# Storing one row of the first tile ahead, through Pool's queue, in a softmax bound by DMA

## The chip, the cores and the metric

One core of a Trainium2 chip. The names are the profile's: DVE is the vector engine, ACT the scalar engine, Pool (POOL) GpSimd and SP the sync engine; SBUF is the memory on the chip, HBM the memory that holds input and output. A transfer is cut into pieces, each one packet record of the trace, which 16 DMA engines move. The metric is device microseconds of one execution, as the median of several; runs of this kernel agree within about 0.3%.

## The reference

```python
x = np.random.randn(32, 512, 1024).astype(np.float32)      # temperature = 0.5
scaled = x / temperature
shifted = scaled - np.max(scaled, axis=-1, keepdims=True)
exp_x = np.exp(shifted)
return exp_x / np.sum(exp_x, axis=-1, keepdims=True)
```

67.1 MB are read and 67.1 MB written, so 134.2 MB must pass the DMA engines, however the arithmetic is done.

## The kernel before

The 16384 rows are cut into 16 tiles of 1024 rows, eight on each of 128 partitions. The eight rows of a partition lie together in HBM and in SBUF, so a whole tile moves in pieces of 32 KiB, and one row of every partition (128 x 4 KiB, 0.52 MB) in pieces of 4 KiB. There are six buffers. SP issues the loads, ACT the stores; a load into a used buffer waits for the store out of it. A tile is computed in "groups" of rows: the first two and last two tiles in two groups of four, the others in one of eight.

```python
def load():
    i = len(tiles)
    if i < len(PASSES):
        xt = data.tile([P, ROWS, d], f32, name="xt")     # data: 6 buffers
        nc.sync.dma_start(out=xt, in_=dram(xf, i))
        tiles.append(xt)

# maximum(g):     DVE reduces the rows of group g to their maxima (L68)
# exponential(g): ACT, row by row, exp and its sum (L77)
# divide(g):      DVE, reciprocal of the sums, then row by row (L95) or whole (L92)

def store(g):
    i, a, k = groups[g]
    if a + k == ROWS:                                    # the tile's last group
        nc.scalar.dma_start(out=dram(of, i), in_=tiles[i])
        load()

for _ in range(BUFS):
    load()
for g in range(len(groups) + 1):
    # ... cut: the last two tiles divide and store ahead of the next maximum
    maximum(g); exponential(g)
    divide(g - 1); store(g - 1)
```

## Time and profile before

| What | Value | Where it is from |
|---|---|---|
| time | 317.11 us, 317.06 to 317.88 in 3 runs; 317.26 us in 6 | the runs |
| DMA queues' busy share | 49.8% loads + 49.2% stores | the page, DMA queues |
| steady DMA rate | 432 to 433 GB/s | busy time by stretches, 60 to 280 us |
| one piece of 32 KiB on one of 16 engines | 1.213 us, 256 on each: 310.5 us | packet records of the trace |
| fullest compute engine | DVE, 79% | the page, busy time |

Read it from the DMA row. A kernel whose transfers run at one rate from the first to the last microsecond has a time of "bytes over rate, plus two ends", and what an engine does beside them matters only where it leaves the transfers without work.

Two sums from the records of data packets: **Slow packets** is the time that pieces took beyond their usual duration (1.213 us for 32 KiB, 1.062 for 28, 0.611 for 16, 0.159 for 4), summed and divided by 16 engines. **Idle** is the time between the first and the last data packet less the time of these packets over 16. In the kernel before they are 2.08 and 0.45 us: 310.53 + 2.08 + 0.45 = 313.06 us, from 1.73 to 314.79.

### The profile page before, as it was taken

Reading aid. Unit: us, or ns where it says so; the run is one execution under the profiler, and the core shown is the slowest. Engines: PE = TensorE matmul, PEld = TensorE weight load, DVE = VectorE, ACT = ScalarE, POOL = GpSimd, SP = SyncE. Lnnn points to the kernel's source line nnn. Section 1 sums busy time; section 2 is a strip of 40 time slices with the busy share of each in tenths; the row PEclk is TensorE's granted clock in tenths of the full one; section 3 lists DMA queues with packets and bytes.
Section 4 is the critical chain, followed back from the end, with each engine's and each line's share of the span. In section 5 each row is a group of like instructions: output and inputs, shape, how many; then the busy total and the mean of one; then the engine's idle time right before and its main releaser. Section 6 shows DMA issues by size and latency. Waiting matters only on the chain. (4 is left out here: it accounts for less than half of the span.)

```text
span 316.0 us, 530 instructions
## 1 busy us (share of the span) xinstructions
DVE 251.0 (79%) x146; ACT 148.1 (47%) x257; POOL 0.2 (0%) x4
## 2 busy tenths in 40 slices
DVE  0399999999689794997939979299793999979710
ACT  0176637680907428083380924708247091564700
POOL 0000000000000000000000000000000000000000
DMA  8999999999999999999999999999999999999996
GB/s 328 415 448 423 377 456 407 460 403 456 408 452 415 452 402 444 419 452 411 452 415 452 427 436 432 431 436 427 436 427 448 415 448 419 448 415 456 407 456 282
DMA packets 4611, 134.24 MB, mean 425 GB/s; under 512 B 512, under 2 KB 512, under 8 KB 512
## 3 DMA queue, kind: packets, MB, share of 16 engines
q1 hardware_dynamic: 2304, 67.11, 49.8%
q10 hardware_dynamic: 2304, 67.11, 49.2%
q14 instruction: 3, 0.02, 0.0%
HBM read 67.11 MB, written 67.11 MB: 425 GB/s over the span
## 5 line engine op out<-in xcount | busy, mean ns | idle before, releaser
L77 ACT ACTIVATE xt<-xt,bias 128x1024 f32<-128x1024 f32 x128 | 145.1, 1135 | 136.7 <-DVE bias L71 127.2
L68 DVE TENSOR_REDUCE top<-xt 128x8 f32<-128x8192 f32 (+1 forms) x20 | 139.5, 6976 | 44.6 <-DMA xt<-in_x_dram 44.6
L95 DVE TENSOR_SCALAR xt<-xt,recip 128x1024 f32<-128x1024 f32 x80 | 54.3, 749 | 0.5
L92 DVE TENSOR_TENSOR xt<-xt,recip 128x8192 f32<-128x8192 f32 x6 | 52.2, 8692 | 0.2
L77 ACT ACTIVATION_READ_ACCUMULATOR xt<-xt,bias 128x1 f32 x128 | 23.8, 186 | 0.0
L77 ACT ACT_TABLE_LOAD x1 | 1.3, 1283 | 13.3 <-DMA xt<-in_x_dram 13.3
L89 DVE RECIPROCAL recip<-sums 128x8 f32<-128x8 f32 (+1 forms) x20 | 3.7, 187 | 4.1 <-ACT xt L77 4.1
L71 DVE TENSOR_SCALAR bias<-top 128x8 f32<-128x8 f32 (+1 forms) x20 | 3.4, 170 | 0.7
L138 POOL MEMSET const-bfloat16-1.0<- 128x1 bf16 x1 | 0.1, 101 | 0.0
L138 POOL MEMSET const-uint8-127<- 128x1 uint8 x1 | 0.1, 101 | 0.0
L138 POOL MEMSET const-float32-0.0<- 128x1 f32 x1 | 0.1, 98 | 0.2 <-issue 0.2
L138 POOL MEMSET const-float32-1.0<- 128x1 f32 x1 | 0.1, 98 | 0.0
## 6 DMA issues: line engine op xcount, KB each, us to landing
xt<-in_x_dram SPq DMA_DIRECT2D x16, 4096.0 KB, 49.7
out_dram<-xt ACTq DMA_DIRECT2D x16, 4096.0 KB, 29.5
```

Source lines behind the costliest of these rows:

```text
L68: nc.vector.tensor_reduce(out=top, in_=tiles[i][:, a : a + k, :], axis=mybir.AxisListType.X, op=extreme)
L71: nc.vector.tensor_scalar_mul(bias, in0=top, scalar1=-scale)
L77: nc.scalar.activation(tiles[i][:, a + b, :], tiles[i][:, a + b, :], mybir.ActivationFunctionType.Exp, bias=bias[:, b : b + 1], scale=scal ...
L89: nc.vector.reciprocal(recip, sums)
L92: nc.vector.tensor_mul(xt, xt, recip.unsqueeze(2).to_broadcast([P, k, d]))
L95: nc.vector.tensor_scalar_mul(tiles[i][:, a + b, :], in0=tiles[i][:, a + b, :], scalar1=recip[:, b : b + 1])
L138: nc = _bacc.Bacc("TRN2", target_bir_lowering=False, num_devices=1)
```

## The change

The intent: until 33 us only loads run, and the first group of the first tile is finished at 25 us. The first row of each partition, 0.52 MB, is stored then, through a third queue, so that writing begins sooner. ACT stores the other seven rows where it stored all eight.

```diff
     def store(g):
         i, a, k = groups[g]
-        if a + k == ROWS:
-            nc.scalar.dma_start(out=dram(of, i), in_=tiles[i])
+        if g == 0:
+            nc.gpsimd.dma_start(out=dram(of, i)[:, :1, :], in_=tiles[i][:, :1, :])
+        elif a + k == ROWS:
+            a = 1 if i == 0 else 0
+            nc.scalar.dma_start(out=dram(of, i)[:, a:, :], in_=tiles[i][:, a:, :])
             load()
```

## The prediction

> **What bounds the kernel now.** I read the head of the page first: which engine is full?
>
> ```profile
> DVE 251.0 (79%) x146; ACT 148.1 (47%) x257; POOL 0.2 (0%) x4
> DMA  8999999999999999999999999999999999999996
> GB/s 328 415 448 423 377 456 407 460 403 456 408 452 415 452 402 444 419 452 411 452 415 452 427 436 432 431 436 427 436 427 448 415 448 419 448 415 456 407 456 282
> q1 hardware_dynamic: 2304, 67.11, 49.8%
> q10 hardware_dynamic: 2304, 67.11, 49.2%
> HBM read 67.11 MB, written 67.11 MB: 425 GB/s over the span
> ```
>
> No compute engine is. The 16 DMA engines are, at 9 tenths in every slice but the first and last; the loads' queue (q1) and the stores' (q10) take 49.8 + 49.2 = 99.0% of the span. So the time is the bytes over the DMA rate, plus the two ends. The slices' rates swing between 402 and 460 because a packet counts where it starts; longer stretches show the rate itself and where it drops:
>
> ```profile
> core 0: us, DVE busy (x) ACT busy (x) POOL busy (x), PEclk, DMA share, GB/s
> 34.00:36.00 2.00, 2.00 (x1) 0.76 (x2) 0.00 (x0) 1.00 1.29 442
> 36.00:38.00 2.00, 1.93 (x4) 0.49 (x1) 0.00 (x0) 1.00 0.74 262
> 38.00:40.00 2.00, 2.00 (x4) 2.00 (x5) 0.00 (x0) 1.00 1.06 426
> 60.00:110.00 50.00, 43.99 (x20) 27.49 (x48) 0.00 (x0) 1.00 1.00 432
> 120.00:280.00 160.00, 133.07 (x70) 77.53 (x135) 0.00 (x0) 1.00 1.00 433
> 33.00:39.00 6.00, 5.93 (x6) 3.25 (x7) 0.00 (x0) 1.00 1.02 371
> 39.00:45.00 6.00, 6.00 (x4) 3.15 (x6) 0.00 (x0) 1.00 1.00 431
> ```
>
> 432 to 433 GB/s is the steady rate, mixed or not. The packet records say the same: 32 KiB (one partition's eight rows) in 1.213 us on one engine. Each engine moves 2 x 128 of them: 256 x 1.213 = 310.5 us. The first packet starts at 1.73 us and the last store lands at 315.15 (packets end at 314.8). That leaves 314.8 - 1.7 - 310.5 = 2.6 us of lost DMA time. I find it in three places: first packets, which take 1.4 to 2.5 us in place of 1.2 (some 0.7 us); the opening of the store queue, where 33:39 moves 371 GB/s in place of 432, so 6 x (1 - 371/432) = 0.85 us; and a few slower load packets near 115 us (about 0.3 us), and the rest over the whole run.
>
> Is compute late for its transfers at the end? The reduce (L68) and the last store say:
>
> ```profile
> 13.28 4.42 DVE L68 TENSOR_REDUCE top<-xt 128x4 f32<-128x4096 f32 x1 [13.28 <-DMA xt<-in_x_dram]
> 22.81 2.74 DVE L95 TENSOR_SCALAR xt<-xt,recip 128x1024 f32<-128x1024 f32 x4
> 25.47 4.42 DVE L68 TENSOR_REDUCE top<-xt 128x4 f32<-128x4096 f32 x1
> 32.86 4.41 DVE L68 TENSOR_REDUCE top<-xt 128x4 f32<-128x4096 f32 x1
> 32.98 0.37 ACTq L102 DMA_DIRECT2D out_dram<-xt  x1
> 284.24 4.41 DVE L68 TENSOR_REDUCE top<-xt 128x4 f32<-128x4096 f32 x1
> 301.13 0.34 ACTq L102 DMA_DIRECT2D out_dram<-xt  x1
> ```
>
> The last tile lands at 282.55 us by its landing record, 1.7 us before its reduce starts. The store before the last lands at 305.52, so when the last one is issued (301.13) the engines still have over 4 us of stores to do. The chain of waits names the computation of the last tiles, but it ends at that issue; what ends the program is the queue behind it, which compute beats by 4 us.
>
> **What the Trainium skill says.** "DMA: Bandwidth & Descriptors", section "Issuing engines are not separate DMA queues": transfers issued by scalar, sync or gpsimd all run on the same 16 engines and interleave. The trace agrees: q1 and q10 sum to 99.0% and neither is faster for being two. So a third queue adds no capacity. Same page, "Specifications": a fabric ceiling of 435 GB/s; 433 is measured here, so the rate is at its end. Same page, "Queues, rings and completion order": an engine goes round its queues packet by packet. The two queues' equal shares agree. "SBUF — State Buffer", section "Who interferes with whom": a DVE tensor_scalar in a two-port mode keeps GpSimd from writing descriptors, a tensor_reduce never does. No DMA of before comes from Pool, so nothing shows that; but L95 takes 749 ns for 1024 elements and the reduce 4408/4 = 1102 ns, so L95 does run in a faster mode.
>
> **The change, part by part.** Removed: 1/8 of the first store of ACT, 128 x 4 KiB = 0.52 MB, 8 pieces on each engine; ACT's pieces for this tile shrink from 32 to 28 KiB. Added: the same 0.52 MB, by Pool, after the first group's divide. No byte, compute instruction or other store moves; the order of DVE, ACT and SP stays as it was, except that the seventh load waits for both partial stores of the first tile.
>
> Bytes: the same, so 310.5 us of engine time stays. Eight more packets per engine: a 32 KiB packet takes 1.213 us and would take 1.205 at 435 GB/s, so at most some 8 ns each of fixed cost, 8 x 8 ns = 0.06 us. An estimate from these, 0.1 us.
>
> When: row 0's divide ends at about 23.6 us, the group's at 25.5. Pool's descriptors come after that (possibly held until the divide ends). The first load began 1.0 us after issue; ACT's first store, behind running loads, 37.0 - 33.0 = 4.0 us. So I expect Pool's first packet at 26 to 30 us, and, taking turns with 1.213 us load packets, 8 x (1.213 + 0.152) = 11 us to finish: about 38 to 41, well before the rest of the store.
>
> Who is delayed: at most 0.52 MB / 432 GB/s = 1.2 us for the loads in flight (third and fourth tile). The third lands at 32.66 and is read at 40.24, the fourth lands at 49.0 and is read at 51.90: 7.6 and 2.9 us of slack. Later ACT has 0.52 MB less ahead of the other stores, so the loads' lag is given back: with two queues in equal turns, total bytes ahead of a given load are the same. ACT's first store is still issued at 33.0 since the DVE order ahead of it needs only tiles 0 and 1.
>
> What it can gain is only idle or slow DMA time, and before 33 us there is none: loads alone run at 433. Storing earlier moves a load later by as much. The one thing in reach is the 0.85 us at the opening of the store queue. If it is a cost of the first store whatever its size, it moves to 27 us and the sum is 0. If small pieces open it more gently, up to -0.85. If each queue's opening costs, Pool's adds up to +0.85. I have no view that decides; I take +0.1 for the packets and +0.1 for the opening: 317.1 + 0.2 = 317.3.
>
> **The rivals.** (1) The early store fills idle write capacity, so that the end comes 0.52 MB = 1.2 us sooner: 315.9. Against it: 433 GB/s of loads alone and 432 of mixed traffic, so there is no spare write side. (2) Pool's queue is costly: descriptors late behind DVE's divides, small pieces that stall a load packet at every turn, say 0.3 us at each of 8 turns (29 load packets near the opening took 1.3 to 2.3 us, so such stalls exist): +2.4 us, 319.5. For it: nothing in the trace shows what a 4 KiB piece does to a load. Against: mixed 32 KiB packets take turns free of loss. (3) Pool's store lands so late that the seventh load waits on it instead of on ACT's (which landed at 57.65): this needs 17 us more than I expect, and even then the sixth load is in flight until 88.12, so the load queue would not run dry; about 317.3.
>
> **Range and chances.** Before's own three times span 317.06 to 317.88, so 0.4 us either way is noise. The opening gives -0.85 to +0.85, rival 2 a tail to +2.4: 316.2 to 318.8. Faster by 2% means below 310.8; with 310.5 us of packets, 1.7 ahead and 1.2 us of launch and end outside (317.1 - 315.9), that cannot be had by reordering: 1%. Slower by 2% means over 323.5, 6.4 us more DMA time from 0.4% of the bytes: 2%. Within: 97%.
>
> **What would show it.** In the changed profile: DMA at 9 tenths throughout, a third queue with 128 data packets and 0.52 MB, steady rate still 432 to 433, the last load still landing about 282.5, ACT's first store still issued at 33.0, last store still 4 us behind its predecessor's landing. Right or wrong on the opening: the rate from 25 to 45 us against before's loss of 0.85 us. I am wrong if load packets beside Pool's pieces are lengthened by tenths of a microsecond each time, if the loads of tiles 3 to 5 come late enough to make DVE wait at 51.9 or 69.5, or if the tail beyond the last store grows because Pool now has a queue to close.

## The result, and the profile after

317.29 us (317.09 to 317.51, 6 runs) against 317.26 (317.06 to 318.08, 6 runs). Here and below a ratio is the mean time of one kernel's runs over that of the other's of the same rounds, so not quite the ratio of the medians quoted. It is 0.9996, 95% interval 0.9983 to 1.0009: nothing gained, nothing lost.

The page of the changed kernel, its DMA strip, its queues with packets, MB and share, and Pool's new row:

```profile
DMA  8999999999999999999999999999999999999996
q1 hardware_dynamic: 2304, 67.11, 49.7%
q10 hardware_dynamic: 2304, 66.59, 48.9%
q0 software_dynamic: 144, 0.52, 0.4%
L104 POOL DMA_DIRECT2D out_dram<-xt x1 | 1.1, 1142 | 23.4 <-DVE xt L95 23.4
```

Pool's queue is there: 144 packets are 128 pieces and 16 semaphore updates, 0.52 MB. Its 0.4% and the 48.9% of the stores add to 49.3%, where the stores alone had 49.2% of a span 0.3 us longer. The share moved from one queue to another.

The same stretches as in the prediction, of the changed kernel:

```profile
33.00:39.00 6.00, 5.93 (x6) 3.25 (x7) 0.00 (x0) 1.00 0.99 371
39.00:45.00 6.00, 6.00 (x3) 3.08 (x6) 0.00 (x0) 1.00 0.97 420
120.00:280.00 160.00, 133.76 (x71) 78.38 (x139) 0.00 (x0) 1.00 1.00 433
```

The last column is GB/s: the steady rate is the same, and so is the hole while the store queue opens. Short stretches count a packet where it starts: two traces of the kernel before gave 371 and 377 for the first of these and 431 and 437 for the second. The packet sums are the better measure.

The order of instructions in time around the start:

```profile
22.75 2.74 DVE L95 TENSOR_SCALAR xt<-xt,recip 128x1024 f32<-128x1024 f32 x4
23.81 1.14 POOL L104 DMA_DIRECT2D out_dram<-xt  x1 [23.36 <-DVE xt L95]
25.41 4.41 DVE L68 TENSOR_REDUCE top<-xt 128x4 f32<-128x4096 f32 x1
32.91 0.38 ACTq L107 DMA_DIRECT2D out_dram<-xt  x1
```

Pool waits for the divide of row 0 alone, starts its issue at 23.81 us and ends it at 24.95, before the group's divide ends at 25.49. The first piece moves at 28.17 us and the last ends at 40.75. In that time each engine's load pieces come later by 8 x 0.159 = 1.27 us. The third load landed at 33.22 us (before: 32.66), the fourth at 50.35 (49.00), the last at 282.40 (282.55). ACT's stores are issued at 32.91, as before at 32.98, and at 300.97, before at 301.13.

Packet sums: slow packets 1.59 us and idle 0.54, against 2.08 and 0.45. Most of the difference is the patch of slow load packets near 115 us in before's trace, which is not in this one.

### The profile page after: what moved, and what is told of

It is laid out like the page before. It is cut to its first block, busy times and chain, and to the rows that moved or that the text cites. A ratio compares the mean times of both kernels' runs of the same rounds, so it can differ in the third digit from the quotient of the medians.

```text
span 315.7 us, 534 instructions
## 1 busy us (share of the span) xinstructions
DVE 251.0 (79%) x146; ACT 148.1 (47%) x257; POOL 1.3 (0%) x5
## 3 DMA queue, kind: packets, MB, share of 16 engines
q10 hardware_dynamic: 2304, 66.59, 48.9%
## 5 line engine op out<-in xcount | busy, mean ns | idle before, releaser
L104 POOL DMA_DIRECT2D out_dram<-xt x1 | 1.1, 1142 | 23.4 <-DVE xt L95 23.4
```

The source lines that it names most:

```text
L104: nc.gpsimd.dma_start(out=dram(of, i)[:, :1, :], in_=tiles[i][:, :1, :])
```

## The experiments

Theory D: the time is the bytes at the engines' rate plus two ends; a store moved ahead takes the place of a load and nothing else changes. It must be told from two rivals that would show the same total. Rival W: the early store does gain its 1.2 us and Pool's queue costs as much, so that the two cancel. Rival C: the chain of computation of the last tiles sets the end, so that early transfers never counted. Beside that, two small questions: what the opening of the store queue costs, and what a small piece costs. Every experiment was timed in 5 rounds beside the kernel before, whose median was 317.27 us in the rounds of the first four and 317.14 in the others. The first four shared one chip, the next four another, the last had a third. The edits of "The row ahead, by ACT", "Four rows ahead, by Pool" and "The row not stored" are against the changed kernel, the others against the kernel before.

### The kernel before, once more

No edit.

> Control: the kernel before, unchanged. Every theory expects a ratio of 1.000, within 0.001. What I want from it is a second trace: if the lost DMA time at the opening of the store queue (33 to 39 us at 371 GB/s in place of 432, 0.85 us) belongs to the program, it is there again, 340 to 395 GB/s; if it was chance, that stretch moves 425 or more. The slow load packets near 115 us (0.3 us) I expect to be chance and gone or elsewhere.

317.08 us, ratio 0.9991 (0.9978 to 1.0005). Stretches, last column GB/s:

```profile
33.00:39.00 6.00, 5.93 (x6) 3.25 (x7) 0.00 (x0) 1.00 0.97 377
```

The hole at the opening belongs to the program; in the packet sums it is 0.56 us in this trace and 0.95 in the first (33 to 40 us), so its size has some chance in it. The patch near 115 us is gone: chance, as expected. The fourth and fifth loads landed at 48.58 and 68.32 us, against 49.00 and 68.77 in the first trace of the very same kernel. Landing times of loads in two traces of one kernel differ by up to 0.7 us (the last load: 282.55 and 281.84) without a cause in the program. The changed kernel's fourth load is 1.35 us later than in the first trace and 1.77 later than in this one.

### The row ahead, by ACT

```diff
-            nc.gpsimd.dma_start(out=dram(of, i)[:, :1, :], in_=tiles[i][:, :1, :])
+            nc.scalar.dma_start(out=dram(of, i)[:, :1, :], in_=tiles[i][:, :1, :])
```

> The same row ahead, but by ACT's queue: no Pool, no software descriptors. Theory D (the time is the bytes at 433 GB/s plus two ends; an early store only takes a load's place): 317.3, ratio 1.000. Rival W (the early store does gain its 1.2 us, and Pool's queue costs as much, so that the two cancel in the change): without Pool the gain shows, 316.1, ratio 0.996. On the opening: if it costs whatever opens ACT's queue, the slow load packets move to 30 us and none are left at 36; if it belongs to the first large store, they stay at 35 to 38 us.

317.49 us, ratio 1.0002 (0.9989 to 1.0015); correct. Rival W wanted 0.996, which is outside. There was no hidden gain for Pool to eat up. On the opening: ACT's first 4 KiB piece moved at 26.73 us with next to no slow load packet beside it (0.02 us); they came at 35 to 40 us (0.62 us), where the 28 KiB pieces began at 38.1. So the cost is not that of opening ACT's queue.

### Four rows ahead, by Pool

```diff
-            nc.gpsimd.dma_start(out=dram(of, i)[:, :1, :], in_=tiles[i][:, :1, :])
+            nc.gpsimd.dma_start(out=dram(of, i)[:, :4, :], in_=tiles[i][:, :4, :])
-            a = 1 if i == 0 else 0
+            a = 4 if i == 0 else 0
```

> Four rows ahead by Pool in place of one: 2.1 MB ahead, still 8 pieces of Pool on each engine (16 KiB each). Theory D: 317.3, ratio 1.000. Rival W: the gain is 4 x 1.2 us and the cost of 8 Pool pieces stays 1.2, so 317.3 - 3.6 = 313.7, ratio 0.989.

317.20 us, ratio 0.9997 (0.9985 to 1.0010); correct. Four times the bytes ahead, and no gain: W's 0.989 is far outside. The slow packets (0.72 us) now came at 25 to 35 us, where Pool's 16 KiB pieces began (29.5), and none when ACT's queue opened at 37.

### Pool for one row of every tile

```diff
         if a + k == ROWS:
-            nc.scalar.dma_start(out=dram(of, i), in_=tiles[i])
+            nc.gpsimd.dma_start(out=dram(of, i)[:, :1, :], in_=tiles[i][:, :1, :])
+            nc.scalar.dma_start(out=dram(of, i)[:, 1:, :], in_=tiles[i][:, 1:, :])
             load()
```

> The first row of each of the 16 tiles goes by Pool, at the time of the tile's store and not ahead: 16 times Pool's pieces, no gain from earliness. Theory D: 128 more packets on each engine at 0.159 + 1.062 - 1.213 = 0.008 us each, 1.0 us in all: 318.3, ratio 1.003. Rival W: 16 x 1.2 = 19 us of cost, 336, ratio 1.06.

317.73 us, ratio 1.0010 (0.9997 to 1.0022); correct. The edit did not do all that I expected of it: Pool's issue waits for its own row alone, so the first tile's row went ahead here too, 9 us before ACT's store (32.69), and so did the second tile's (38.37 against 51.74):

```profile
23.59 1.14 POOL L102 DMA_DIRECT2D out_dram<-xt  x1 [23.15 <-DVE xt L95]
```

Queues (packets, MB, share) of this kernel:

```profile
q10 hardware_dynamic: 2304, 58.72, 43.1%
q0 software_dynamic: 2304, 8.39, 6.5%
```

Sixteen times Pool's work costs 0.5 us by the medians, and the interval includes no cost at all. W's cost of 1.2 us for each is dead: it would be 19 us, less 1.2 for the row that went ahead. D's number was missed as well: 1.003 lies just outside the interval. Its 1.0 us is there in the packet sums (311.55 us of usual packet time against 310.53), but the idle sum fell from about 0.4 to 0.0 and gave half of it back: small pieces overlap a little in the records, so that a sum of their durations says too much. Pool's queue as such has no price that can be seen here.

### The row not stored

```diff
         if g == 0:
-            nc.gpsimd.dma_start(out=dram(of, i)[:, :1, :], in_=tiles[i][:, :1, :])
+            pass
```

> As the changed kernel, but the first row of each partition of the first tile is not stored at all (wrong result on purpose). Theory D: 8 pieces of 0.159 us fewer on every engine, 1.27 us less: 316.0, ratio 0.996. Rival C (the chain of computation of the last tiles sets the end, and early bytes do not matter): 317.3, ratio 1.000.

315.91 us, ratio 0.9958 (0.9946 to 0.9971); wrong result. 317.14 - 315.91 = 1.23 us for 8 x 0.159 = 1.27 us of pieces. Half a megabyte at the very beginning is felt in full at the end, 275 us later. That is the plainest evidence for D against C: pieces at the very beginning count in full.

### No computation

```diff
-            if g < len(groups):
-                maximum(g)
-                exponential(g)
-            if g > 0 and not alone:
-                divide(g - 1)
-                store(g - 1)
+            if g > 0:
+                store(g - 1)
```

(and the division ahead of the last tiles goes too)

> No computation: each tile is loaded and stored as it is (wrong result on purpose), with the same transfers and the same six buffers; the first store comes at 13 us in place of 33. Theory D: the same 310.5 us of packets between the same ends: 316.5, between 315.5 and 317.5, ratio 0.995 to 1.001. Rival C: with no chain of computation the time falls by over 2%, below 311. Rival W: stores 20 us earlier fill idle write capacity, also well below 315.

316.67 us, ratio 0.9983 (0.9971 to 0.9996); wrong result. From the page of the copying kernel:

```profile
GB/s 333 404 395 458 408 462 404 462 404 462 404 462 404 462 404 462 404 462 404 462 404 462 404 462 404 462 404 462 404 462 404 462 404 462 404 462 404 462 404 333
HBM read 67.11 MB, written 67.11 MB: 426 GB/s over the span
```

In the first line the slices read 404 and 462 in turn, 433 on average; the second has the whole span with its two ends. Taking all computation away, and storing from 13 us on in place of 33, saves 0.5 us of 317. So 0.17% is all that waiting for computation costs in this order of transfers; other orders were not tried. Under C the time would have fallen by over 2%. Slow packets are there as ever (0.67 us at the start, 0.84 us at 15 to 20 us, where this kernel's stores open).

### The first tile whole, by Pool

```diff
         if a + k == ROWS:
-            nc.scalar.dma_start(out=dram(of, i), in_=tiles[i])
+            queue = nc.gpsimd if i == 0 else nc.scalar
+            queue.dma_start(out=dram(of, i), in_=tiles[i])
             load()
```

> The whole first tile is stored by Pool in 32 KiB pieces at the time ACT stored it; ACT's queue opens with the second tile at 52 us. Theory D: 317.3, ratio 1.000. On the opening: if the first store of the program costs the 0.85 us, load packets are slow once, near 37 us; if each queue's opening costs it, they are slow again at 54 to 58 us and the time is 318.1, ratio 1.003.

317.39 us, ratio 1.0006 (0.9994 to 1.0019); correct. Stretches, last column GB/s:

```profile
35.00:41.00 6.00, 5.93 (x8) 3.70 (x7) 0.00 (x0) 1.00 1.03 393
54.00:60.00 6.00, 6.00 (x1) 4.17 (x8) 0.00 (x0) 1.00 1.01 437
```

Slow packets worth 0.72 us at 35 to 40 us, when Pool's 32 KiB pieces began, and none at 55.9, when ACT's queue did. The opening is paid once in a program, by the first large store pieces, whichever queue they come by.

### Every store in 4 KiB pieces

```diff
-            nc.scalar.dma_start(out=dram(of, i), in_=tiles[i])
+            for r in range(3):
+                nc.scalar.dma_start(out=dram(of, i)[:, r::3, :], in_=tiles[i][:, r::3, :])
```

> Every store in 4 KiB pieces by ACT: three transfers a tile, of rows 0 3 6, 1 4 7 and 2 5, so that no two rows of a partition join. 1024 store pieces on each engine in place of 128. Theory D with 8 ns a piece: 1024 x 0.159 - 128 x 1.213 = 7.5 us more: 324.8, ratio 1.024, and each piece takes 0.159 us. If pieces cost nothing: 317.3. If every small piece also stalled a load by a tenth of a microsecond (my second rival of the prediction): tens of us more.

334.07 us, ratio 1.0535 (1.0521 to 1.0550); correct. My number was wrong: 16.9 us more in place of 7.5. The pieces did take 0.16 us each, and their usual time sums to 318.08 us on each engine, the 7.5 us more that I had counted. The other 8.5 us of the longer span (332.0 against 316.0) are slow packets (6.77 us in place of 2.08) and idle time (4.23 in place of 0.45). The slow packets are spread over the run from 60 us on. The idle time is not: 1.1 us of it lies at 300 to 304 us and 6.0 at 314 to 322, and before that the sum is below zero, as records overlap. From the page of this kernel, and a stretch near its end:

```profile
GB/s 316 442 442 430 423 434 434 375 421 435 419 406 422 387 456 391 418 393 432 438 393 438 396 436 426 388 440 381 450 425 372 458 382 422 419 416 354 357 163 343
q10 hardware_dynamic: 17152, 67.11, 49.9%
314.00:318.00 4.00, 2.33 (x6) 3.04 (x6) 0.00 (x0) 1.00 0.09 37
```

The hole near the end is a wait for computation, which the kernel before has not: the last tile's divide runs until 320 us, its stores are issued from 319.40 on, and those of the tile before had landed by 315.64. In the kernel before, the last store was issued 4 us before its predecessor landed. So for this kernel, though not for the changed one, C's mechanism holds.

By the packet records, between 40 and 60 us loads moved 378 GB/s and stores 52. An engine that takes one piece from each queue in turn gives 32 KiB to the loads for 4 KiB to the stores, 8 to 1, near the 7.2 measured. After that the two swing for the rest of the run, which fits loads that run ahead until no buffer is free and then leave the engines mostly to stores: 102 and 292 GB/s from 90 to 100 us, 318 and 91 from 100 to 110. ACT's issues were held up too, as its stores' own row of instructions shows (duration in ns, least, median and most):

```profile
L103 ACTq DMA_DIRECT2D out_dram<-xt x48: 378/1206/15229, 32.2 to 320.5; - x48
```

### Loads and stores in 4 KiB pieces

The edit above, and for the loads:

```diff
-            nc.sync.dma_start(out=xt, in_=dram(xf, i))
+            for r in range(3):
+                nc.sync.dma_start(out=xt[:, r::3, :], in_=dram(xf, i)[:, r::3, :])
```

> Why did 4 KiB store pieces cost 16.9 us and not 7.5? Here the loads too go in 4 KiB pieces (the same three transfers of rows 0 3 6, 1 4 7, 2 5). Theory T (turns go by packet: a 4 KiB store piece against a 32 KiB load piece gives loads most of the engine until the buffers run out; then the queues run one at a time, and packets are slow and engines idle at each swing): with equal pieces the turns are equal again and what is left is 1024 more pieces x 0.008 us on each side: 317.2 + 2 x 7.5 = 332.3, no more than this kernel of half the pieces took, with an idle time of the engines below 1 us and slow packets worth 1.5 us as in the kernel before. Rival P (each 4 KiB piece simply costs 16.9/896 = 0.019 us more): twice the pieces, twice the cost, 317.2 + 33.8 = 351. Rival I (ACT's issues of three transfers a tile hold up its own computation): the delay of over 9 us of the store-only version stays, 341 or more.

331.00 us, ratio 1.0437 (1.0422 to 1.0451); correct. Twice the small pieces, and 3 us faster. Queues, stretches and ACT's issues of this kernel:

```profile
q1 hardware_dynamic: 17152, 67.11, 50.0%
q10 hardware_dynamic: 17152, 67.11, 49.7%
40.00:60.00 20.00, 19.93 (x10) 11.65 (x22) 0.00 (x0) 1.00 1.02 420
120.00:280.00 160.00, 124.10 (x66) 77.67 (x136) 0.00 (x0) 1.00 1.02 421
L104 ACTq DMA_DIRECT2D out_dram<-xt x48: 378/379/6988, 32.7 to 317.7; - x48
```

The rate is steady again, 420 to 421, below 433: small pieces cost rate. From 40 to 60 us loads and stores moved 210 GB/s each. From 100 to 110 they moved 341 and 74, and the rate held at 420, so a swing by itself need not cost. Slow packets are 1.83 us. The idle sum is below zero, but only because the records of one engine overlap by 2%; it hides a hole like the last kernel's, 5.2 us at 312 to 318:

```profile
314.00:318.00 4.00, 2.92 (x5) 0.23 (x2) 0.00 (x0) 1.00 0.13 54
```

So the agreement with my 332.3 is in part luck. An estimate: 134.2 MB at 421 in place of 433 GB/s are 8.8 us, which with the hole's 5.2 make 14.0, where 13.9 were measured. That is about 5 ns for each of the 1792 more pieces of an engine, not 8.

The per-piece price P is refuted (351 expected). Three issues a tile mostly do not hold ACT up (median 379 ns), but rival I is not quite dead: the longest issue, 6.99 us at 281.26, stands in the chain that ended last, ahead of the hole. Unequal pieces do cost: with equal ones the slow packets fell from 6.77 to 1.83 us and the time by 3 us, at twice the small pieces. What else made the ragged kernel slow, buffers running out, ACT stuck in issues (up to 15.2 us each) or the late last tile, these two runs do not separate.

No version beat the kernel before by more than its noise, save those that left out work.

## Why the prediction was right

**The bound.** Right. The sum of 310.5 us of packets plus ends held in both traces; taking 1.27 us of packets away took 1.23 us off, and taking all the computation away took off 0.5. One term was mis-sized: launch and end outside the span are 1.74 us and not 1.2, since the trace is that of an execution of 317.74 us and not of the median. And the equal shares of the two queues, which the prediction takes to agree with turns by the packet, come from equal bytes in any case; turns show in the 378 and 52 GB/s of unequal pieces.

**Bytes and pieces.** Right by the records: 8 ns a piece, 0.06 us; those of the changed kernel give 310.59 us of usual packet time against 310.53. In time it is rather half: 0.46 us for 128 more pieces with Pool's sixteen stores, 4 ns each, and about 5 with small pieces everywhere. Both are far below what the change could show.

**When and who is delayed.** First piece predicted at 26 to 30 us, measured 28.17; end predicted at 38 to 41, measured 40.75. Loads late by at most 1.2 us: the third was later by 0.56 us than in the first trace of the kernel before and by 0.83 than in the second, the fourth by 1.35 and 1.77, so that the bound was passed by 0.2 to 0.6. The slack in DVE covered both, and the reduces at 40 and 52 us did not wait. The prediction had not reckoned with the fifth load, whose slack was the least: it landed at 69.42 us (before: 68.77), 0.05 us ahead of its reduce at 69.47. That the lag is given back later is not shown: the last load landed 0.15 us earlier than in one trace of the kernel before and 0.56 later than in the other.

**The opening.** I left it open between -0.85 and +0.85 and took +0.1. It was near zero: 4 KiB pieces open the store direction at almost no cost (0.08 us of slow packets from 28 to 31 us; 0.02 when ACT sent them), and the first large pieces, now of 28 KiB, pay as before (0.74 us from 33 to 40; 0.95 and 0.56 in two traces of the kernel before, 0.71 with the row not stored). That the cost waits for large pieces I had not thought of. That it is paid once is shown by moving it, to 29 us with Pool's 16 KiB pieces and to 17 with no computation, and by Pool's whole tile, with which it came at 37 us by Pool's queue and not again by ACT's. What in the engine it is, stays open. Only load packets are lengthened, and most before a store piece moves: in the first trace of the kernel before, 21 of the 29 slow ones had started when the first store piece did, at 37.02 us.

**The rivals.** Idle write capacity (315.9) and costly Pool pieces (319.5) fell both, and their cancelling was excluded separately, with the row ahead by ACT and with sixteen rows by Pool. The seventh load did not wait on Pool's store, which landed at 43.38 us, but on ACT's, at 56.08.

**The size.** 317.3 predicted, 317.29 measured. The 0.2 us above 317.1 are within the noise of before's own median, so the agreement to a hundredth is luck; that it could be neither 315.9 nor 319.5 is not.

## What to carry to other kernels

Before moving a transfer earlier, look whether the DMA engines have anything idle or slow to fill at that time: here loads alone already ran at the full rate, and an early store only traded places with a load. Removing a little work at the start, on purpose and with a wrong result, tells in one run whether early bytes count at the end; removing all computation tells what waiting for it costs. And keep the pieces of queues that run side by side alike in size, and large: beside 32 KiB pieces the queue of 4 KiB pieces got 52 GB/s against 378, and 4 KiB in both still cost 13.9 us. When a sum of idle time is small or negative, look where in the run it lies: here it hid a hole of 5 us.

## What the Trainium skill lacked or had wrong

- "DMA: Bandwidth & Descriptors", section "Queues, rings and completion order", says that an engine goes round its queues by packets. It lacks the consequence: a queue of 4 KiB pieces beside one of 32 KiB got 52 GB/s against 378, and the kernel took 334.07 us, while 4 KiB pieces on both sides took 331.00.
- No page that I read has the cost of the first large store after loads alone: 0.56 to 0.95 us of slow load packets, once in a program, by whichever queue it comes, with 4 KiB pieces nearly free of it.
- Same page, section "Measured (HBM→SBUF, 128 partitions, SWDGE, issued from GpSimd)", gives sums by transfer size and a time by the packet for its smallest transfer alone; it has no duration for pieces of 4 to 32 KiB. Here one engine took 0.159 us for a piece of 4 KiB and 1.213 for one of 32 KiB, some 8 ns a piece beyond the bytes; in the time of the kernel 4 to 5 ns of it were left.
- "SBUF — State Buffer", section "Who interferes with whom", says that tensor_scalar in a two-port mode and GpSimd block each other, whichever issues first. It can't be seen for sure here: with one row of every tile by Pool, nine of the sixteen issues began inside divides by rows (the second at 38.37 us, within 37.30 to 40.05) and took 0.53 us, as did four with DVE idle. One, at 263.05, just ahead of a divide, took 0.96. The first issue of the changed kernel, beside divides, took 1.14 us; first issues beside a reduce took 0.66, so half a microsecond may be that lock. Spans on Pool are rough.
